# B's attention as a near part of two blocks and a far part by remainders of four, o by rows, p not divided

## The chip, the cores and the metric

One core of a Trainium2 chip runs the kernel. The time is the device time of one execution in microseconds (us); lower is better. The engines have names in the profile: PE is TensorE (matrix products and transposes), PEld its weight load, DVE is VectorE, ACT is ScalarE, POOL is GpSimd, SP is SyncE, which here issues every DMA.

## The reference

One decoder block over 1024 tokens of width 1024, in float32. Two mixers share one input projection; their outputs are normed, joined and projected; then an MLP of width 4096 follows.

```
proj = (rms_norm(x) * (1 + sc_a) + sh_a) @ w_in         # width 2304
A: 8 query heads on 2 key heads of 64; query t sees keys t-127..t; a sink logit joins the denominator
B: 8 heads of 64; three branches (128, 1), (512, 4), (2048, 16):
   branch (w, d): query t attends keys t, t-d, ..., t-(w//d)*d
   outputs are joined with weights proportional to the branches' softmax denominators
mixed = concat(rms_norm(oa), rms_norm(ob)); y = mixed @ w_out
x = x + gt_a * rms_norm(y)
h = rms_norm(x) * (1 + sc_m) + sh_m
x = x + gt_m * rms_norm(relu(h @ w_up)**2 @ w_down)
```

Since the branches are joined by their denominators, B is one softmax over all keys in which a key counts once for each branch that has it.

## The kernel before, in words

Every float32 product is made of pairs of a high and a low part (names with `hl`, `oh`/`ol`, `ph`), most with three matmuls. A planner written in the kernel itself goes through all steps ahead of time with costs of its own (`op`, `pe_op`, `load`), and so fixes the order of instructions on each engine; `prefer` orders the kinds of TensorE's steps. On the chip each engine runs its list in that order.

The stages of the program are, in the profile's time: loads and the first unit (0 to 46 us); the input projection in six units of 384 columns (units 0 to 3 hold two heads of B each, units 4 and 5 hold four query heads and one key head of A), each over eight blocks of 128 tokens, with attention between the projection matmuls (46 to 436); the output projection over eight token blocks (436 to 546); a transition (546 to 574); the MLP (574 to 1136) and a tail. The projection's matmuls are L766, L767 and L769 (`pj`). After a tile, `evac` splits v (`v_hl`), applies the rotary turn, and transposes q (`pq`, L719) and k (`pk`, L731) to `qt` and `kt`.

B's attention (`s_b`) takes one head and two query blocks at a time and all key blocks up to them: scores (L1022), a mask that adds the logarithm of how many branches have the key (L1040, with the minimum `mn` of the negated scores), exp with its sum `den` (ACT, L1047), the reciprocal (DVE, L1050), and the division of p (POOL, L1052). A's (`s_a_`) does the same for four heads and two key blocks, with the sink (L1101 to L1107) and the division at L1111 on POOL or DVE. `t_pv` transposes p (L1125, L1128 for B, L1132 for A), splits it into `ph` (ACT L1139, DVE L1143), and multiplies with v as the weights: the columns that stream are the queries, so o comes out with its head dimension on the partitions (B: L1156, L1159, L1161; A: L1167). High and low halves are added (L1187 and L1191, L1202 and L1207) and o goes to DRAM.

The output projection (`out_block`) loads o (L1318), splits it (`oh` L1331, `ol` L1334), squares it and sums over the partitions with `pm_o` (L1347) for the two norms `rab`, and multiplies with w_out (L1373 to L1375); then the post-norm, the residual and the pre-norm of the MLP (`xn`, L1427) and its transposes (`px`, L1436). `kring`, `qring`, `vring` are the rings of buffers of keys, queries and v; `Res` counts their places.

Of the kernel before, what the change touches and what calls it, by code (L numbers as in the profile page):

```python
# [57 lines left out]
CW_MB = HEAD  # L58
CW_MA = CW_MB + 1024
CW = CW_MA + 256  # L60


def _host(inputs):

    h = {n: np.ascontiguousarray(inputs[n]) for n in _INS}
    c = np.zeros((P, CW), np.float32)
    c[:, CW_C:CW_C + KC] = inputs["c"][0].reshape(P, KC)
    c[:, CW_SINK:CW_SINK + 8] = inputs["sink_a"]
    b = inputs["b_ada"][0].reshape(48, P)
    c[:, CW_COL:CW_COL + 56] = np.concatenate(  # L70
        [inputs["g_attn_pre"][0].reshape(8, P), inputs["g_mlp_pre"][0].reshape(8, P), b[0:16], b[24:40],
         inputs["g_mix_a"][0].reshape(4, P), inputs["g_mix_b"][0].reshape(4, P)]).T
    h["positions"] = np.ascontiguousarray(inputs["positions"][0].reshape(TB, P).T)
    _constants(c)
    h["consts"] = c
    return h


def _constants(c):
    c[:, CW_ID:CW_ID + P] = np.eye(P, dtype=np.float32)  # L80
    p = np.arange(P)[:, None]
    d = p + 896 - np.arange(1024)[None, :]
    mult = ((d >= 0) & (d <= 128)).astype(int)
    mult += (d >= 0) & (d <= 512) & (d % 4 == 0)
    mult += (d >= 0) & (d % 16 == 0)
    neg = np.array([BIG, 0.0, -np.log(2.0), -np.log(3.0)], np.float32)
    c[:, CW_MB:CW_MB + 1024] = neg[mult]
    d = p + P - np.arange(256)[None, :]
    c[:, CW_MA:CW_MA + 256] = np.where((d >= 0) & (d <= 127), 0.0, BIG)
    c[:, CW_F:CW_F + 8] = np.array(INV_FREQ, np.float32)[None, :]  # L90
# [217 lines left out]
def hybrid_block(ctx: ExitStack, tc: tile.TileContext, x, positions, w_ada, b_ada, g_attn_post, w_in, w_out,  # L308
# [33 lines left out]
    WR, WS, NP, NV, NK, NQ, NT, NO = 10, 5, 4, 21, 10, 12, 2, 6  # L342
# [4 lines left out]
    r_v, r_k, r_q, r_p, r_ph, r_ot, r_tmp = Res(NV), Res(0), Res(0), Res(NP), Res(NT), Res(NO), Res(1)  # L347
# [20 lines left out]
    nsink = const.tile([P, 8], F32, name="nsink")  # L368
    ssq = const.tile([P, TB], F32, name="ssq")
# [4 lines left out]
    o_dram = [dram.tile([KC, P, 256], F32, name=f"o_dram{i}") for i in range(4)]  # L374
# [16 lines left out]
    class Tok:  # L391
        pass

# [269 lines left out]
    toks, kts, e_posted = {}, {}, {}  # L663
    acc_at = [(pj, "pj", r_pj)] * 2 + [(po, "o", r_o)] + [(psp, "s", r_s)] * 2 + [(pt, "t", r_t)] * 2 + [(px, "x", r_x)]

    def evac(u, tb, get_ps, done, r_bank):
# [6 lines left out]
        t.v = []  # L673
        b = {}

        def f_vh():
            t.v += [vring.tile([P, 2, 64], F32R, name="v_hl", tag="v") for _ in range(nv)]
            for h in range(nv):
                A.copy(t.v[h][:, 0], get_ps()[:, n + 64 * h:n + 64 * h + 64])
        e2 = op("ACT", nv * t_as(64), f_vh, [done], takes=[(r_v, nv)], prio=2)  # L680

        def f_vl():
            for h in range(nv):
                V.tensor_tensor(t.v[h][:, 1], get_ps()[:, n + 64 * h:n + 64 * h + 64],
                                t.v[h][:, 0].bitcast(F32), ALU.subtract)
        t.e_v = op("DVE", nv * t_dv(64), f_vl, [e2], prio=2)
# [27 lines left out]

        def f_pq():
            t.q = [qring.tile([P, P], F32R, name="qt", tag="qt") for _ in range(nq)]
# [3 lines left out]
        e7 = pe_op("post", 0.056 * nq, f_pq, [e6, e_idr], takes=[(r_x, 1), (r_q, nq)])  # L720

        def f_q():
            for h in range(nq):
                A.mul(t.q[h][:], b["pq"][:, h].bitcast(F32), -0.125)
        t.e_q = op("ACT", nq * t_ps(128), f_q, [e7], gives=[(r_x, 1)], prio=2)

        def f_pk():
            b["pk"] = px.tile([P, 4, P], F32R, name="pk", tag="x")
# [3 lines left out]
        need_k = (2 if tb % 2 == 0 else 0) if u < 4 else (2 if tb == 0 else 1 if tb < TB - 1 else 0)  # L732
        e8 = pe_op("post", 0.112 * nk, f_pk, [e6], takes=[(r_x, 1), (r_k, need_k)], gives=[(r_sp, 1)])

        def get_k(i, h):
            if (u, i, h) not in kts:
                kts[u, i, h] = kring.tile([P, 2, 256], F32R, name="kt", tag="kt")
            return kts[u, i, h]

        def f_k(fn):  # L740
            def f():
                for h in range(nk):
                    kt = get_k(tb // 2, h) if u < 4 else get_k(tb, 0)
                    o = tb % 2 * P if u < 4 else P
                    fn(kt[:, :, o:o + P], b["pk"][:, 2 * h:2 * h + 2].bitcast(F32))
            return f

        def posted():
            st.posted = u * TB + tb + 1
        twice = u >= 4 and tb < TB - 1  # L750
        t.e_k = op(("ACT", "DVE"), (nk * t_ps(256), nk * t_dv(256)), (f_k(A.copy), f_k(V.tensor_copy)), [e8],
                   gives=[] if twice else [(r_x, 1)], prio=2, after=posted)
        t.e_kn = None
        if twice:
            def f_kn(fn):
                return lambda: fn(get_k(tb + 1, 0)[:, :, 0:P], b["pk"][:, 0:2].bitcast(F32))
            t.e_kn = op(("ACT", "DVE"), (t_ps(256), t_dv(256)), (f_kn(A.copy), f_kn(V.tensor_copy)), [t.e_k],
                        gives=[(r_x, 1)], prio=2)
# [98 lines left out]
    def open_attention():  # L857
        if e_rope.t is None or any(x.t is None for x in e_hl.values()):
            return False
        nonlocal kring, qring, pprob, pth, opool, adp, mask_a, mask_b, e_mask  # L860
# [4 lines left out]
        qring = pool("qring", NQ, **kw)  # L865
        pprob = pool("pprob", NP, **kw)
        pth = pool("pth", NT, **kw)
        opool = pool("op", NO, **kw)
        adp = pool("adp", 1, **kw)
        r_k.give(sc.clk["PE"], NK)  # L870
        r_q.give(sc.clk["PE"], NQ)
        masks = mkp.tile([P, 1280], F32, name="masks")
        e_mask = load(lambda: nc.sync.dma_start(masks[:], consts[:, CW_MB:CW_MB + 1280]), 655360, prio=-20)
        mask_b = masks[:, 0:1024]
        mask_a = masks[:, 1024:1280]
# [4 lines left out]
    kring = qring = pprob = pth = opool = adp = mask_a = mask_b = e_mask = None  # L880
# [84 lines left out]
    def feed_ada():  # L965
        if st.d > 1.0 + ada.i * 4.1 / NADA and ada.i < NADA:
# [5 lines left out]
    items = [(u, tp, h) for u in range(4)  # L972
             for tp, h in ((0, 0), (0, 1), (1, 0), (1, 1), (2, 0), (3, 0), (2, 1), (3, 1))]
    items += [(u, qb) for u in (4, 5) for qb in range(TB)]
    UB = 2 * (0.218 * 20 + 0.107 * 36 + 0.43 * 10)
    UA = 0.86 * 8 + 0.43 * 15 + 0.43 * 15

    def need(it):
        return it[0] * TB + (2 * it[1] + 2 if it[0] < 4 else it[1] + 1)

    def count(it):
        return it[1] + 1 if it[0] < 4 else (2 if it[1] else 1)
# [3 lines left out]

    def emit_item(i):
        it = items[i]
        rec = Tok()
        rec.p = []  # L990
        (s_b if it[0] < 4 else s_a_)(i, it, rec)
        nch = count(it)
        for ch in range(nch):
            t_pv(i, it, rec, ch, nch)

    def s_b(i, it, rec):
        u, tp, h = it
        shared = tp < 2
        rec.e_p = []
        rec.held = 1 if shared else 2  # L1000
        for qi in range(2):
            qb = 2 * tp + qi
            W = (qb + 1) * P
            last_mn = None
            b = {}
            for c0 in range(0, W, 512):
                m = c0 // 512
                cw = min(512, W - c0)
                end = c0 + cw == W

                def f_s(c0=c0, cw=cw, m=m, qi=qi, qb=qb, W=W, b=b):
                    if m == 0:
                        if qi == 0 or not shared:
                            rec.tile = pprob.tile([P, 1024], F32, name="p_sb", tag="p")
                        off = 2 * tp * P + P if shared and qi else 0
                        rec.p.append(rec.tile[:, off:off + W])
                        b["mn"] = small.tile([P, 2], F32, name="mn", tag="mn")
                    s = b["s", m] = psp.tile([P, 512], F32, name="s_ps", tag="s")
                    for b0 in range(0, cw, 256):
                        w = min(256, cw - b0)  # L1020
                        for hl in range(2):
                            T.matmul(s[:, b0:b0 + w], toks[u, qb].q[h][:],  # L1022
                                     kts[u, (c0 + b0) // 256, h][:, hl, :w], start=(hl == 0), stop=(hl == 1))
                d = 0.218 * -(-cw // 256)
                deps = [toks[u, j].e_k for j in range(2 * tp, 2 * tp + 2)] + [toks[u, qb].e_q]
                slot = 1 if m == 0 and (qi == 0 or not shared) else 0
                done = end and qi == 1

                def after(d=d, done=done):
                    progress(d, it)  # L1030
                    if done:
                        st.s_items = i + 1
                gives = []
                if done:
                    gives = [(r_q, 2)] + ([(r_k, 4)] if tp == 3 else [])
# [939 lines left out]
```

## Time and profile before

| what | value |
|---|---|
| runs | 1173.84 us median of 3 (1173.43 to 1175.96) |
| profiled execution | 1175.14 us, of which the span is 1173.3 |
| granted TensorE clock, mean | 0.993 |
| busy: PE, DVE, ACT, POOL | 1137.0, 871.9, 677.6, 239.3 us |
| projection and attention | 46 to 436 us |
| output projection, transition | 436 to 546, 546 to 574 us |
| MLP | 574 to 1136 us |

An engine's share is its busy time over the span. A line of a group has the source line, the engine, the operation, what it writes and reads, the shapes, the count, then busy us and mean ns, then idle time ahead of it and what ended that. A row of the timeline has its start, its length and the count of like instructions in it. A matmul's recorded length holds its pipeline, so two neighbouring ones overlap.

### The profile page before, as it was taken

Reading aid. Unit: us, or ns where it says so; the run is one execution under the profiler, and the core shown is the slowest. Engines: PE = TensorE matmul, PEld = TensorE weight load, DVE = VectorE, ACT = ScalarE, POOL = GpSimd, SP = SyncE. Lnnn points to the kernel's source line nnn. Section 1 sums busy time; section 2 is a strip of 40 time slices with the busy share of each in tenths; the row PEclk is TensorE's granted clock in tenths of the full one; section 3 lists DMA queues with packets and bytes.
Section 4 is the critical chain, followed back from the end, with each engine's and each line's share of the span. In section 5 each row is a group of like instructions: output and inputs, shape, how many; then the busy total and the mean of one; then the engine's idle time right before and its main releaser. Section 6 shows DMA issues by size and latency. Waiting matters only on the chain.

```text
span 1173.3 us, 17394 instructions
## 1 busy us (share of the span) xinstructions
PE 1137.0 (97%) x6042; PEld 987.6 (84%) x6042; DVE 871.9 (74%) x1765; ACT 677.6 (58%) x1421; POOL 239.3 (20%) x295
## 2 busy tenths in 40 slices
PE   8999999999999999999899999999999999999996
PEld 7889999999988878887688888888888888888885
DVE  7876787776788896668969764499653796636998
ACT  7966676666666786666667524473225733246542
POOL 2053464554654451112000000000000000000002
PEclk9999999999999999999999999999999999999998
DMA  9712234132223224465485147922258411575103
GB/s 327 209 64 78 74 87 117 53 104 71 70 70 104 79 73 130 172 202 218 150 333 181 36 150 243 357 84 90 100 214 306 143 50 54 202 283 201 37 19 144
DMA packets 96488, 166.54 MB, mean 142 GB/s; under 512 B 11408, under 2 KB 48400, under 8 KB 96400
## 3 DMA queue, kind: packets, MB, share of 16 engines
q1 hardware_dynamic: 96400, 165.42, 42.0%
q8 instruction: 48, 0.79, 0.3%
q14 instruction: 40, 0.33, 0.1%
HBM read 137.08 MB, written 28.31 MB: 141 GB/s over the span
## 4 chain that ended last, share of the span: by engine, by line
PE 77%; DVE 11%; issue 4%; ACT 3%; POOL 1%; DMA 1%; DVEq 0%; POOLq 0%; SPq 0%; ACTq 0%
PE mlp_ps L1798 16%; PE mlp_ps L1799 16%; PE mlp_ps L1797 16%; PE pj L766 4%; PE pj L767 4%; PE pj L769 4%; PE s_ps L1022 3%; PE o_ps L1156 2%; PE pt_ps L1125 1%; DMA w_st<-in_w_in 1%; PE y_ps L1373 1%; PE y_ps L1375 1%; PE y_ps L1374 1%; PE s_ps L1073 1%; PE pt_ps L1128 1%
## 5 line engine op out<-in xcount | busy, mean ns | idle before, releaser
L1797 PE MATMUL mlp_ps<-hw 128*128 128x512 f32 x896 | 349.7, 390 | 1.1 <-ACT hw L1559 1.1
L1798 PE MATMUL mlp_ps<-hw 128*128 128x512 f32 x896 | 348.7, 389 | 1.1 <-DVE hw L1565 1.1
L1799 PE MATMUL mlp_ps<-hw 128*128 128x512 f32 x896 | 348.6, 389 | 0.0
L1797 PEld LDWEIGHTS mlp_ps<-hw 128*128 128x128 f32 x896 | 168.2, 188 | 36.9 <-ACT hw L1559 1.6
L1798 PEld LDWEIGHTS mlp_ps<-hw 128*128 128x128 f32 x896 | 168.2, 188 | 36.6 <-DVE hw L1565 1.4
L1799 PEld LDWEIGHTS mlp_ps<-hw 128*128 128x128 f32 x896 | 168.2, 188 | 34.9
L1568 DVE TENSOR_TENSOR hw<-w,hw 128x1024 fp32r<-128x1024 f32 x96 | 114.6, 1219 | 95.1 <-ACT hw L1561 93.0
L1561 ACT CAST hw<-w 128x1024 fp32r<-128x1024 f32 x96 | 97.4, 1046 | 129.9 <-PE mlp_ps L1799 93.2
L1897 POOL TENSOR_TENSOR st<-st,nhalf 128x1 f32<-128x1 f32 x8 | 7.7, 977 | 602.0 <-DVE st L1895 602.0
L766 PE MATMUL pj<-w_hl,hw 128*128 128x384 f32 x320 | 119.1, 372 | 0.0
L767 PE MATMUL pj<-w_hl,hw 128*128 128x384 f32 x320 | 108.7, 340 | 0.5 <-DVE w_hl L506 0.5
L769 PE MATMUL pj<-w_hl,hw 128*128 128x384 f32 x320 | 108.9, 340 | 0.0
L1561 ACT CAST hw<-u 128x1024 fp32r<-128x1024 f32 x48 | 48.6, 1052 | 64.6 <-PE mlp_ps L1799 64.6
L1143 DVE TENSOR_TENSOR ph<-pt_ps,ph 128x512 fp32r<-128x512 f32 (+1 forms) x110 | 68.9, 644 | 18.6 <-ACT ph L1139 18.0
L1568 DVE TENSOR_TENSOR hw<-u,hw 128x1024 fp32r<-128x1024 f32 x48 | 57.0, 1218 | 18.2 <-ACT hw L1561 18.2
L1139 ACT CAST ph<-pt_ps 128x512 fp32r<-128x512 f32 (+1 forms) x110 | 59.8, 562 | 12.9 <-PE pt_ps L1128 8.8
L1052 POOL TENSOR_SCALAR p_sb<-p_sb,den 128x128 f32<-128x128 f32 (+3 forms) x64 | 49.1, 773 | 87.4 <-DVE den L1050 49.8
L1855 DVE TENSOR_TENSOR yacc<-yacc,mlp_ps 128x512 f32<-128x512 f32 x96 | 62.2, 681 | 3.3 <-PE mlp_ps L1799 3.3
L767 PEld LDWEIGHTS pj<-w_hl,hw 128*128 128x128 f32 x320 | 61.0, 191 | 2.1 <-DVE w_hl L506 0.8
L766 PEld LDWEIGHTS pj<-w_hl,hw 128*128 128x128 f32 x320 | 60.7, 190 | 1.6 <-issue 0.5
L769 PEld LDWEIGHTS pj<-w_hl,hw 128*128 128x128 f32 x320 | 60.6, 189 | 0.0
L1047 ACT ACTIVATE p_sb<-p_sb,mn 128x128 f32<-128x128 f32 (+3 forms) x64 | 50.0, 782 | 17.4 <-DVE mn L1040 13.5
(206 smaller groups left out, 2201.0 us busy)
## 6 DMA issues: line engine op xcount, KB each, us to landing
hw<-s_dram SPq DMA_DIRECT2D x84, 512.0 KB, 4.4
wa_st<-in_w_ada SPq DMA_DIRECT2D x32, 512.0 KB, 4.2
w<-in_w_up SPq DMA_DIRECT2D x32, 512.0 KB, 5.1
w<-in_w_down SPq DMA_DIRECT2D x32, 512.0 KB, 7.5
s_dram<-hw SPq DMA_DIRECT2D x28, 512.0 KB, 4.5
x_sb<-in_x SPq DMA_DIRECT2D x16, 512.0 KB, 5.4
wa<-in_w_ada SPq DMA_DIRECT2D x32, 256.0 KB, 6.1
w_st<-in_w_in SPq DMA_DIRECT2D x32, 192.0 KB, 3.8
```

The lines of the kernel that those rows point to most:

```text
L766: T.matmul(ps, hw[:, tb, 0, t], w[:, 0], start=(k == 0), stop=False)
L767: T.matmul(ps, hw[:, tb, 0, t], w[:, 1], start=False, stop=False)
L769: T.matmul(ps, hw[:, tb, 1, t], w[:, 0], start=False, stop=(k == KC - 1))
L1047: A.activation(rec.p[qi], rec.p[qi], AF.Exp, bias=b["mn"][:, m:m + 1], scale=-1.0, accum_out=b["den"][:])
L1139: A.copy(b["ph"][:, 0, :w], b["pt"][:, :w])
L1143: V.tensor_tensor(b["ph"][:, 1, :w], b["pt"][:, :w], b["ph"][:, 0, :w].bitcast(F32), ALU.subtract)
L1561: A.copy(out[j][0], flat(src[j]))
L1568: V.tensor_tensor(out[j][1], flat(src[j]), out[j][0].bitcast(F32), ALU.subtract)
L1797: T.matmul(ps[m][:], sh, mh, start=starts and k == 0, stop=False, **kw)
L1798: T.matmul(ps[m][:], sh, ml_, start=False, stop=False, **kw)
L1799: T.matmul(ps[m][:], sl, mh, start=False, stop=k == 3, **kw)
L1855: e = op("DVE", t_dv(512), lambda: V.tensor_tensor(y(), y(), ps[m][:], ALU.add), [e, ml.e_y[tb, n]], gives=gives, prio=1)
```

## The change

Within each block of 128 tokens the rows are ordered by their remainder of four: the rows of x and of the output are loaded and stored so, and the positions and masks are made for it. B's keys are then held in one tile of 2048 columns for half of the tokens (512), by remainder, so that a remainder's 128 keys of a half lie side by side.

B's softmax is cut in two parts, each with its own minimum and sum. The near part of a query block has its own and the previous block (branch 1: 15 blocks of keys a head). The far part takes 128 queries of one remainder in a half of the sequence, against the keys of the same remainder of that half and of the one before (branches 2 and 3, 12 blocks a head). Before there were 36 a head. v of B is stored to DRAM and loaded again by remainder (`v_dram`, `vf`), the far queries stand in a tile `qf`.

p is no longer divided. In p times v the block of p is now the weight, and v streams: 128 columns (high and low of v) for the high part of p, 64 for the low one, for each head and key block, so that o comes out by rows of tokens. The sums of the far part go through DRAM (`fs_dram`), `far_weights` and `a_weights` make factors `wts` for each row and head, and the output projection multiplies o by them, adds the far part, and transposes o (`pxo`) for w_out. The sums of squares come from ACT's accumulation, without `pm_o`. The rings become smaller, the junk tile of the squares goes, and the tile of `xn` is taken at the post-norm's squares instead.

```diff
-    WR, WS, NP, NV, NK, NQ, NT, NO = 10, 5, 4, 21, 10, 12, 2, 6
+    WR, WS, NP, NV, NK, NQ, NF, NT, NO = 10, 4, 4, 8, 3, 6, 2, 2, 3
...
-            nc.sync.dma_start(x_t[tb][:], x[tb * P:(tb + 1) * P])
+            nc.sync.dma_start(x_t[tb][:], rows(x, tb))
...
+                nc.sync.dma_start(v_dram[u][half_][:, 32 * c:32 * c + 32],
+                                  t.v[:].rearrange("p h s d -> p (h s d)").bitcast(F32))
+                    nc.sync.dma_start(vfs[ub][:].bitcast(F32), v_dram[u][half_][:].rearrange("r p n -> p r n"))
...
-            e = op("DVE", 0.08, lambda b=b: V.reciprocal(b["den"][:], b["den"][:]), [e], prio=0)
-            rec.e_p.append(op("POOL", t_pts(W),
-                              lambda b=b, qi=qi: G.tensor_scalar(rec.p[qi], rec.p[qi], b["den"][:], 1.0,
-                                                                 ALU.mult, ALU.mult), [e], prio=1))
...
-                for s2 in range(2):
-                    T.matmul(o[:, :256], v0, ph[:, s2, 0:256], start=(ch == 0 and s2 == 0), stop=False)
...
-                for s2 in range(2):
-                    T.matmul(o[:], vv, ph[:, s2], start=(ch == 0 and s2 == 0), stop=(last and s2 == 1))
...
+            for ci in range(2):
+                for kb in range(r.nk):
+                    v = r.v(kb, ci)
+                    kw = dict(stop=kb == r.nk - 1, skip_group_check=True)
+                    T.matmul(rec.o[:, 2 * j + ci], b["ph"][:, 0, at(kb, ci)], v.rearrange("p s d -> p (s d)"),
+                             start=kb == 0, **kw)
+                    T.matmul(rec.o[:, 2 * j + ci, 0:64], b["ph"][:, 1, at(kb, ci)], v[:, 0], start=False, **kw)
...
+        e1 = op("DVE", t_dv(D), by_head(V, lambda: b["ot"][:], wts[:, tb, 0:16]), [el, e_wb, e_wa[tb]], prio=2)
...
+                    T.transpose(b["po", g][:, k], b["ot"][:, kk * P:kk * P + P], ident)
...
-        if st.d < 5.99 and st.d - st.a < LEAD:
+        if st.d < 5.99 and st.d - st.a < (LEAD if st.d < 5 else 0.2):
```

TensorE in the A stage, before: one item's p times v (L1167, two matmuls for a key block with the columns of four heads), between transposes of p (L1132) and scores (L1073).

```order
L766 MATMUL pj<-w_hl,hw 128x384
L767 MATMUL pj<-w_hl,hw 128x384
L769 MATMUL pj<-w_hl,hw 128x384
L1132 MATMUL pt_ps<-head,p_sb 128x128 x4
L1073 MATMUL s_ps<-kt,qt 128x256 x8
L1167 MATMUL o_ps<-ph,v_hl 128x512 x2
L1132 MATMUL pt_ps<-head,p_sb 128x128 x4
L1167 MATMUL o_ps<-ph,v_hl 128x512 x2
```

TensorE in the A stage, after: p times v of half an item, two heads and two key blocks, in pairs of L1180 (high part of p) and L1182 (low part); L748 is the transpose of q and L811 to L814 are the projection.

```order
L748 MATMUL pq<-ident_r,sp 128x128 x4
L1180 MATMUL o_ps<-v_hl,ph 128x128
L1182 MATMUL o_ps<-v_hl,ph 128x64
L1180 MATMUL o_ps<-v_hl,ph 128x128
L1182 MATMUL o_ps<-v_hl,ph 128x64
L1180 MATMUL o_ps<-v_hl,ph 128x128
L1182 MATMUL o_ps<-v_hl,ph 128x64
L1180 MATMUL o_ps<-v_hl,ph 128x128
L1182 MATMUL o_ps<-v_hl,ph 128x64
L811 MATMUL pj<-w_hl,hw 128x384
```

Where four matmuls of 512 columns served the two key blocks of an item's four heads, sixteen of 128 and 64 columns now do.

DVE in the A stage, before: between the masks of one item (L1089) stand the sink and the reciprocal of the item ahead (L1101, L1106, L1107), on which its division by POOL or DVE (L1111) and then its transposes wait.

```order
L1143 TENSOR_TENSOR ph<-pt_ps,ph 128x512
L1101 TENSOR_TENSOR es_5789<-mn_5692,head 128x4
L1143 TENSOR_TENSOR ph<-pt_ps,ph 128x512
L1089 ISA p_sb,mn_5782<-s_ps,masks,nsink 128x128
L1089 ISA mn_5782 128x1
L1106 TENSOR_TENSOR den_5693<-den_5693,es_5789 128x4
L1107 RECIPROCAL den_5693<-den_5693 128x4
```

DVE in the A stage, after: the sink and the reciprocal make `wts` (L1262, L1266, L1267) for the output projection.

```order
L1262 TENSOR_TENSOR wts<-mn,head 128x8
L1170 TENSOR_TENSOR ph<-pt_ps,ph 128x512
L1266 TENSOR_TENSOR wts<-wts,den 128x8
L1267 RECIPROCAL wts<-wts 128x8
L1170 TENSOR_TENSOR ph<-pt_ps,ph 128x512
```

They stand among the same splits of p, but no step of the item's own attention waits for them now, and no L1111 is left.

More of the change, by code (lines that the diff above doesn't have):

```diff
@@ L713, in evac @@
         e6 = op("DVE", t_dv(64 * nq) + t_dv(128 * nk), f_l, [e5, t.e_v], gives=[(r_bank, 1)], prio=2)
+        first = isb and ub not in e_qf
+        new_k = first if isb else tb == 0
+        e_qf.setdefault(ub, [])
         def f_pq():
-            t.q = [qring.tile([P, P], F32R, name="qt", tag="qt") for _ in range(nq)]
+            t.q = [qring.tile([P, 2, P], F32R, name="qt", tag="qt") for _ in range(nq // 2)]
+            if first:
+                qfs[ub] = qfring.tile([P, 2, 4, P], F32R, name="qf", tag="qf")
             b["pq"] = px.tile([P, 4, P], F32R, name="pq", tag="x")
@@ L1133, in t_pv @@
-        d = w / P * 0.113
-        et = pe_op("t", d, f_t, rec.e_p, takes=[(r_t, 1), (r_ph, 1)],
-                   gives=[(r_p, rec.held)] if last else [], after=lambda: progress(d, it))
+            b["pt"] = pt.tile([P, 512], F32, name="pt_ps", tag="t")
+            for kb in range(r.nk):
+                for ci in range(2):
+                    T.transpose(b["pt"][:, at(kb, ci)], r.p[:, ci, r.k0 + kb * P:r.k0 + kb * P + P], ident)
+        d = 0.216 * r.nk
+        et = pe_op("t", d, f_t, r.e_p, takes=[(r_t, 1), (r_ph, 1)], gives=[(r_p, 1)], after=lambda: progress(d, it))
@@ L1180, in t_pv @@
+        if not j:
             return
         ob = {}
[L1182 to L1217 removed]
@@ new lines, in f_o, with f_st @@
+        def f_o():
+            ob["o"] = opool.tile([P, 4, 64], F32, name="ot", tag="ot")
+            A.copy(ob["o"][:], rec.o[:, :, 0:64])
+        e = op("ACT", t_ps(256), f_o, [ep], takes=[(r_ot, 1)], prio=0)
+        e = op("DVE", t_dv(256), lambda: V.tensor_tensor(ob["o"][:], ob["o"][:], rec.o[:, :, 64:128], ALU.add), [e],
+               gives=[(r_o, 1)], prio=0)
+        u, kind = it[:2]
+        both = []
+        for x_ in range(1 if kind == "a" else 2):
+            def f_st(x_=x_):
+                o = ob["o"][:] if kind == "a" else ob["o"][:, 2 * x_:2 * x_ + 2]
+                if kind == "a":
+                    to = o_dram[it[2]][:, 256 * (u - 4):256 * (u - 4) + 256]
+                elif kind == "n":
+                    to = o_dram[2 * it[2] + x_][:, 512 + P * u:512 + P * u + P]
+                else:
+                    to = of_dram[it[2]][2 * it[3] + x_, :, P * u:P * u + P]
+                nc.sync.dma_start(to, o.rearrange("p h d -> p (h d)"))
+            key = (it[2] if kind == "a" else 2 * it[2] + x_ if kind == "n" else ("f", it[2]), i, x_)
+            e_o[key] = load(f_st, 131072 if kind == "a" else 65536, [e], prio=-5,
+                            gives=[(r_ot, 1)] if kind == "a" or x_ else [])
@@ L1338, in f_sum @@
-        def f_sum():
-            sq = b["sq"] = b["ot"].rearrange("p (a b) t -> p a b t", a=2)
-            V.tensor_tensor(sq[:, :, 0:2], sq[:, :, 0:2], sq[:, :, 2:4], ALU.add)
-            V.tensor_tensor(sq[:, :, 0], sq[:, :, 0], sq[:, :, 1], ALU.add)
-        e = op("DVE", t_dv(512) + t_dv(256), f_sum, [e], prio=2)
-        def f_pm():
-            b["pm"] = px.tile([P, 2], F32, name="pm_o", tag="x")
-            for i in range(2):
-                T.matmul(b["pm"][:, i:i + 1], b["sq"][:, i, 0], ones[:, 0:1], start=True, stop=True)
-            b["rab"] = small.tile([P, 2], F32, name="rab", tag="rab")
```

589 lines of the change are left out of this document (308 added, 281 removed).

## Prediction

> **What bounds the kernel now.** I read the page's busy times first, then the chain that ended last, then the busy time of each engine by stage, the waits of TensorE, and last the timeline where single matmuls can be priced.
>
> ```profile
> PE 1137.0 (97%) x6042; PEld 987.6 (84%) x6042; DVE 871.9 (74%) x1765; ACT 677.6 (58%) x1421; POOL 239.3 (20%) x295
> ...
> PE 77%; DVE 11%; issue 4%; ACT 3%; POOL 1%; DMA 1%; DVEq 0%; POOLq 0%; SPq 0%; ACTq 0%
> ```
>
> TensorE is busy for 97% and carries 77% of the chain, so the first question is what the change does to TensorE's own work, and the second how much of its idle time can go. By stage (length, then busy us of PE, weight load, DVE, ACT, POOL, then granted clock and DMA share):
>
> ```profile
> 46.00:345.00 299.00, 293.41 (x2076) 282.73 (x2074) 220.30 (x763) 199.94 (x605) 155.39 (x177) 0.99 0.29 81
> 345.00:436.00 91.00, 83.04 (x525) 77.15 (x523) 80.52 (x267) 68.50 (x227) 43.84 (x59) 0.96 0.28 83
> 436.00:546.00 110.00, 107.63 (x527) 88.13 (x526) 74.70 (x136) 74.07 (x125) 18.74 (x30) 1.00 0.50 169
> 546.00:574.00 28.00, 23.05 (x107) 18.48 (x107) 25.23 (x40) 18.18 (x29) 4.91 (x2) 1.00 0.25 101
> 574.00:1136.00 562.00, 561.65 (x2474) 464.33 (x2475) 402.50 (x420) 267.00 (x355) 0.00 (x0) 1.00 0.48 168
> ...
> 150.00:325.00 175.00, 173.17 (x1245) 167.56 (x1243) 126.71 (x431) 112.09 (x334) 103.26 (x111) 1.00 0.30 83
> ```
>
> The rows are: projection with B's attention, with A's attention, output projection, transition, MLP. The change touches nothing in the MLP. Up to 546 TensorE idles 5.6 us (299.00 - 293.41), 8.0 us and 2.4 us; the transition idles 5.0 us. The clock columns add what a busy TensorE loses: 0.01 of 299 and 0.04 of 91, 3.0 + 3.6 = 6.6 us. In the A stage DVE is busy 80.5 of 91 us, nearly as long as TensorE. The longest waits up to 546 and the one of the transition:
>
> ```profile
> PE pq L719 <- DVE sp L711: 3.7, 3, 2.2
> PE o_ps L1167 <- ACT p_sb L1094: 2.1, 1, 2.1
> PE o_ps L1167 <- DVE ot L1207: 2.0, 1, 2.0
> ...
> 560.28 1.09 PE L1436 MATMUL px<-head,xn 128*128 128x128 f32 x8 [3.05 <-ACT xn L1427]
> ```
>
> The first three are of the A stage and wait for DVE or for what feeds it; each is followed by a stretch of lower clock.
>
> **The price of a TensorE instruction.** A matmul's recorded duration (390 ns for 512 columns) holds its pipeline; the price is the distance from start to start in a full stream.
>
> ```profile
> 376.26 0.62 PE L1167 MATMUL o_ps<-ph,v_hl 128*128 128x512 f32 x2
> 376.72 0.34 PE L766 MATMUL pj<-w_hl,hw 128*128 128x384 f32 x1
> ...
> 377.25 0.64 PE L1073 MATMUL s_ps<-kt,qt 128*128 128x256 f32 x4
> 377.73 0.45 PE L719 MATMUL pq<-ident_r,sp 128*128 128x128 f32 x4
> ...
> 380.33 0.60 PE L1132 MATMUL pt_ps<-head,p_sb 128*128 128x128 f32 x4
> 380.69 0.42 PE L766 MATMUL pj<-w_hl,hw 128*128 128x384 f32 x1
> 380.95 0.33 PE L767 MATMUL pj<-w_hl,hw 128*128 128x384 f32 x1
> 381.12 0.34 PE L769 MATMUL pj<-w_hl,hw 128*128 128x384 f32 x1
> ...
> 382.81 0.56 PE L1073 MATMUL s_ps<-kt,qt 128*128 128x128 f32 x4
> 383.20 0.39 PE L766 MATMUL pj<-w_hl,hw 128*128 128x384 f32 x1
> 383.43 0.34 PE L767 MATMUL pj<-w_hl,hw 128*128 128x384 f32 x1
> ...
> 230.68 0.95 PE L928 MATMUL ada_ps<-ones,ada_acc 128*128 128x1 f32 x8
> 231.49 0.36 PE L1022 MATMUL s_ps<-kt,qt 128*128 128x256 f32 x1
> ```
>
> 512 columns: 0.46 / 2 = 0.23 us. 256 columns: 0.48 / 4 = 0.12. Four transposes: 0.36, and the matmul behind them takes 0.26 where the next takes 0.17, so 0.45 / 4 = 0.11. Four of 128 columns: 0.39, with 0.23 against 0.17 behind them, 0.45 / 4 = 0.11. And eight of a single column: 0.81 / 8 = 0.10. So below 256 columns a matmul does not get cheaper: one column costs what 128 cost. Each has a weight load of its own (6042 of both kinds on the page), and that is what is left to set the price.
>
> The Trainium skill, "TensorE: Matmul & The Clock Gate", section "LDWEIGHTS (loading the stationary operand)", gives a load time of about 107 ns for 128 columns, which these rows bear out; its section "Back-to-back issue gap" gives about 81 ns for a matmul of 128 columns, which they do not.
>
> **The change, term by term.** The counts of before that change:
>
> ```profile
> L1022 PE MATMUL s_ps<-kt,qt 128*128 128x256 f32 x256 | 44.7, 293 | 0.0
> L1156 PE MATMUL o_ps<-ph,v_hl 128*128 128x256 f32 x160 | 36.2, 301 | 2.6 <-DVE ph L1143 2.2 <-DVE ot L1191 0.3
> L1125 PE MATMUL pt_ps<-head,p_sb 128*128 128x128 f32 x160 | 31.5, 278 | 0.4 <-DVE sk L712 0.4
> L1128 PE MATMUL pt_ps<-head,p_sb 128*128 128x128 f32 x128 | 27.3, 275 | 0.0
> L1167 PE MATMUL o_ps<-ph,v_hl 128*128 128x512 f32 x60 | 20.2, 424 | 4.1 <-ACT p_sb L1094 2.1 <-DVE ot L1207 2.0
> L1161 PE MATMUL o_ps<-ph,v_hl 128*128 128x256 f32 x96 | 19.2, 282 | 0.0
> L1073 PE MATMUL s_ps<-kt,qt 128*128 128x256 f32 x112 | 18.6, 292 | 0.1
> L1132 PE MATMUL pt_ps<-head,p_sb 128*128 128x128 f32 x120 | 17.3, 272 | 0.0
> L1022 PE MATMUL s_ps<-kt,qt 128*128 128x128 f32 x64 | 11.1, 255 | 0.0
> L1159 PE MATMUL o_ps<-ph,v_hl 128*128 128x128 f32 x64 | 11.0, 254 | 0.0
> ...
> L1347 PE MATMUL pm_o<-ones,o_sb 128*128 128x1 f32 x32 | 4.5, 243 | 1.2 <-ACT xn L1427 0.4 <-DVE o_sb L1341 0.3
> ...
> L1073 PE MATMUL s_ps<-kt,qt 128*128 128x128 f32 x16 | 2.2, 262 | 0.0
> ```
>
> *TensorE.* Before: 624 of 256 columns (256 + 112 + 160 + 96) x 0.12 = 74.9; 144 of 128 columns (64 + 64 + 16) x 0.11 = 15.8; 60 x 0.23 = 13.8; 408 transposes of p x 0.11 = 44.9; 32 x 0.11 = 3.5. Together 152.9 us. After, by the program: 208 scores of 256 columns = 25.0; 256 scores of 128 columns = 28.2 (64 of near keys, 192 of far); p times v in 336 matmuls of 128 columns = 37.0 and 336 of 64 columns = 37.0; 336 transposes of p = 37.0 and 64 new ones of o in the output projection = 7.0. Together 171.2 us. So B has a quarter fewer key blocks (27 for 36 a head), yet TensorE's work grows by 18.3 us. The reason is the form: v was the weight and one load served 256 or 512 columns of queries; now a block of p is the weight and serves 128 or 64 columns. For A, which is computed over the same blocks, p times v alone goes from 13.8 to 120 x 0.11 + 120 x 0.11 = 26.4 us. The 64-column form is not in the trace; its ends are 0.10 (one column) and 0.11 (128), which moves the sum by 3.4 us. It is on the path everywhere, since TensorE is the bound.
>
> *Idle time of TensorE.* What can be won back by an easier DVE, ACT and POOL is the idle up to 436, 5.6 + 8.0 = 13.6, and the clock, 6.6: 20.2 us. Some idle stays: the calm stretch of 150 to 325 has 1.8 us in 175, about 1%, which over 390 us is 4.1. I take 20.2 - 4.1 = 16.1 us won. From below it could be nothing, if the new, shorter items wait in other places; from above 27.6, if the 7.4 us of output projection and transition go too. I take a value towards the upper side because DVE loses these, and two dozen smaller groups, with nothing of like size in their place before 436:
>
> ```profile
> L1111 DVE TENSOR_SCALAR p_sb<-p_sb,den 128x256 f32<-128x256 f32 x9 | 7.7, 894 | 0.1
> ...
> L1050 DVE RECIPROCAL den<-den 128x1 f32<-128x1 f32 x64 | 9.8, 156 | 8.7 <-ACT p_sb L1047 8.7
> ...
> L1052 POOL TENSOR_SCALAR p_sb<-p_sb,den 128x128 f32<-128x128 f32 (+3 forms) x64 | 49.1, 773 | 87.4 <-DVE den L1050 49.8
> ```
>
> *Costed at nothing.* The 0.16 + 0.77 us of reciprocal and division leave the way from exp to transpose; projection matmuls stand there now and hide it (no row has PE waiting for POOL's p_sb), so removing it gains only through the idle above. SP gets 482 issues for 428: 32 stores of v, 8 reloads of 512 KB, the exchange of far sums. In the order 79 TensorE instructions stand between the last key transposes of the first half and the first matmul on reloaded v, at least 79 x 0.10 = 7.9 us; DMA's share is 0.29 there. Uncovered, each of the 8 reloads could stop TensorE for some us, with scores and projection queued behind it in the fixed order. The exps of B come in more pieces, but ACT is busy 200 of 299 us. In the output projection DVE gets a multiply of 1024 and additions instead of a split and sums; at 74.7 of 110 us it has room, and without it a few us would show. The tile of xn is taken earlier; the last block's 3.05 us wait stays, give or take 1.
>
> *Sum.* 18.3 - 16.1 = +2.2 us. The profiled execution took 1175.14 us (span 1173.3), 1.3 over the median of the runs; on the median, 1173.84 + 2.2 = 1176.
>
> **Rivals.**
> (a) The short matmuls cost less in the new bursts than the nearest rows: with the 64-column form at half of the 128-column one, 336 x 0.055 = 18.5 us go and the time is 1176 - 18.5 = 1157.5. For it: bursts of equal matmuls are longer than before. Against it: eight single columns in a row took 0.10 each. By the skill's 81 ns for both short forms the sum would be lower by (928 - 144) x 0.029 = 22.7 us, an estimate from that page, 1153.
> (b) Faster, by one mechanism: DVE was what held TensorE. With it relieved no wait up to 436 is left, the clock never drops, and the ends of output projection and transition gain some. Between 20.2 and 27.6 us are won back, 1173.84 + 18.3 - 24 = 1168. It decides once over 20.6 us are won. For it: the waits of 2 us name DVE, and 80.5 of 91 us is a full engine. Against it: 5.0 us of the transition end in the chain of the last output block (ACT xn L1427), which keeps its steps.
> (c) Clearly slower: the won-back time is half, 8 us or less, because in a fixed order each p-times-v burst waits for the low part of p (the 2.2 us at L1156 do so today), because the ring of keys has three places, or because reloaded v comes late: 1173.84 + 18.3 - 8 = 1184, and 1192 with nothing won.
> (d) That the change doesn't do what it says I can exclude by the counts of the order.
>
> **How the numbers follow.** No change can be told within about 0.2%, 2.3 us, so 1171.5 to 1176.2. My forecast, 1176 with its own range of 1172 to 1180, gets 0.40 (0.25 of it inside the 0.2%, 0.15 slower), (a) 0.08, (b) 0.24, (c) 0.28. Faster: 0.08 + 0.24 = 0.32; same 0.25; slower 0.15 + 0.28 = 0.43. The range for 8 in 10 goes from the lower part of (b), 1165, to the middle of (c), 1188; outside lie (a) and the end of (c).
>
> **What would show it.** TensorE's instructions of B and A at 0.11 us in the new p-times-v bursts (0.44 us for two pairs) show the price right; 0.3 us or less shows (a). The A stage's idle and clock: 1% idle and 1.00 is my forecast, 8 us idle is (c). DVE in that stage should be well under 80 of 91 us. Waits of matmuls on reloaded v (vf) should be absent. The prediction fails most simply if the projection-and-attention part ends before its old 436 us, or more than 10 us later.

## The result, and the profile after

The changed kernel takes 1301.54 us (median of 4 runs, 1294.7 to 1511.47) against 1173.99: a ratio of 1.1064, 95% interval 1.1019 to 1.1109. Timed again beside the experiments it was 1294.8 against 1175.42, 1.1033 (1.0979 to 1.1087). The forecast was 1176, 1165 to 1188. A ratio with its interval is estimated from single runs and can differ a little from the quotient of the medians. One of the four runs, 1511.47 and the one profiled with the first result, had a clock of about 0.75 from end to end, so the ratio leaves it out and the profile shown below is of another execution of the same kernel, 1306.67 us.

The page's busy times and its row of the granted clock, after:

```profile
PE 1186.3 (91%) x6310; PEld 1039.9 (80%) x6310; DVE 833.1 (64%) x1677; ACT 671.0 (51%) x1448; POOL 176.4 (14%) x195
...
PEclk7698899999999988787899999999999999999995
```

TensorE went from 97% to 91% busy. Its own work grew, as forecast, but that is not where some 120 us went: it idles at the start, and again in the output projection, where the clock row shows a second valley. By stage (length, busy PE, weight load, DVE, ACT, POOL, clock, DMA share), after:

```profile
0.00:106.00 106.00, 74.08 (x362) 65.87 (x363) 58.40 (x143) 57.09 (x97) 16.50 (x27) 0.81 0.51 159
106.00:474.00 368.00, 364.29 (x2653) 357.81 (x2652) 235.48 (x874) 238.28 (x776) 119.88 (x119) 0.97 0.36 106
...
474.00:652.00 178.00, 131.39 (x591) 108.00 (x590) 77.52 (x144) 76.79 (x166) 26.47 (x39) 0.82 0.35 115
652.00:1275.00 623.00, 616.23 (x2710) 508.23 (x2708) 455.62 (x507) 297.42 (x408) 12.51 (x9) 0.99 0.45 160
1275.00:1305.00 30.00, 0.30 (x2) 0.00 (x0) 6.06 (x12) 1.45 (x4) 1.08 (x2) 0.56 0.24 94
```

The stages are cut at the last matmul of each kind in the timeline: of the first unit (`acc`), of the projection (`pj`), of the output projection (`y_ps`), of the MLP (`mlp_ps`). The table has the lengths between these for all kernels, in us of the profiled execution (for the changed kernel one of 1306.67 us and for b_perm8 one of 1203.36, both above the median), and the median of the runs. The kernels were timed in four groups, each beside its own runs of before (1175.42, 1173.87, 1173.78 and 1175.87).

| kernel | to last acc | to last pj | to last y_ps | to last mlp_ps | to the end | median |
|---|---|---|---|---|---|---|
| before | 71.2 | 356.5 | 116.1 | 619.7 | 9.7 | 1173.84 |
| changed | 106.1 | 368.2 | 177.9 | 622.9 | 29.8 | 1294.8 |
| a_x4 | 79.3 | 366.6 | 173.5 | 622.6 | 29.0 | 1274.2 |
| a_all4 | 77.8 | 369.4 | 127.3 | 622.4 | 17.4 | 1215.9 |
| b_perm (4) | 105.6 | 355.6 | 116.2 | 619.7 | 9.7 | 1208.7 |
| b_perm8 | 97.8 | 356.1 | 116.2 | 621.7 | 9.7 | 1194.4 |
| b_perm16 | 78.8 | 353.5 | 116.2 | 620.6 | 9.7 | 1179.5 |
| a_nat | 71.5 | 360.0 | 129.1 | 623.3 | 10.2 | 1196.2 |
| a_nat_lo128 | 72.1 | 360.4 | 127.7 | 622.4 | 10.2 | 1195.7 |
| b_pvA | 72.1 | 360.2 | 118.3 | 620.6 | 9.7 | 1182.8 |
| a_xtnat | 105.7 | 367.6 | 135.6 | 623.9 | 29.8 | 1261.7 |
| a_far4 | 104.3 | 358.8 | 156.5 | 623.8 | 29.1 | 1279.7 |
| a_nat_early | 71.4 | 360.6 | 124.0 | 622.5 | 10.2 | 1190.7 |

Changed against before, in order: +34.9, +11.7, +61.8, +3.2, +20.1, together 131.6 us, the difference of the two spans (the medians are 119.4 apart). Start, output projection and end have 117 of it, and in each of them there are transfers that put rows in the order of the remainder. What TensorE waits for in the changed kernel, with the longest ones:

```profile
PE pxo L1409 <- DVE rs_t L1481: 29.6, 6, 10.8
PE pxt L599 <- ACT x_sb L591: 25.2, 3, 10.6
PE pxo L1409 <- DVE ph L1170: 9.3, 1, 9.3
PE pxo L1409 <- DVE o_sb L1388: 6.5, 1, 6.5
```

The second row is the start: the transposes of x wait for x. The other three are the new transposes of o. The engine that a row names is here only the last in the queue: rs_t is a short step that DVE does just ahead. What the transposes lack is the far part, by the far tile's own waits and its waiters (two lines of that tile's view; the first is its buffer waiting for the transfer, the second its multiply on POOL waiting):

```profile
  DMA far_sb<-of_dram: 66.7, 8
...
  POOL far_sb L1388: 65.1, 7
```

And at the end the queue that issues the transfers takes 25.42 us for nine stores of the output, after, where the last eight before lie within 10.78 us, most of it between the issues (0.33 us for each issue; after, eight of the nine take 2.4 to 4.9 us):

```profile
1267.70 25.42 SPq L1975 DMA_DIRECT2D out_x<-x_sb  x9
```

```profile
1159.79 10.78 SPq L1905 DMA_DIRECT2D out_x<-x_sb  x8
```

### The profile page after: what moved, and what is told of

Read it like the earlier page. It is cut to its first block, busy times and chain, and to the rows that moved or that the text cites. A ratio compares the mean times of both kernels' runs of the same rounds, so it can differ in the third digit from the quotient of the medians.

```text
span 1509.7 us, 17759 instructions
## 1 busy us (share of the span) xinstructions
PE 1425.1 (94%) x6310; PEld 1125.6 (75%) x6310; DVE 846.5 (56%) x1677; ACT 676.1 (45%) x1448; POOL 170.6 (11%) x195
## 4 chain that ended last, share of the span: by engine, by line
PE 85%; DMA 8%; DVE 2%; SPq 1%; issue 1%; ACT 1%; POOL 0%; DVEq 0%; POOLq 0%; ACTq 0%
PE mlp_ps L1867 16%; PE mlp_ps L1869 16%; PE mlp_ps L1868 16%; PE pj L811 5%; PE pj L814 4%; PE pj L812 4%; DMA far_sb<-of_dram 4%; PE s_ps L1126 4%; PE o_ps L1180 3%; PE pt_ps L1160 3%; DMA wa<-in_w_ada 3%; PE o_ps L1182 2%; PE y_ps L1444 1%; PE y_ps L1445 1%; PE y_ps L1443 1%; PE pk L783 1%
## 5 line engine op out<-in xcount | busy, mean ns | idle before, releaser
L1867 PE MATMUL mlp_ps<-hw 128*128 128x512 f32 x896 | 411.7, 459 | 2.0 <-ACT hw L1629 2.0
L1868 PE MATMUL mlp_ps<-hw 128*128 128x512 f32 x896 | 409.8, 457 | 1.5 <-DVE hw L1635 1.5
L1869 PE MATMUL mlp_ps<-hw 128*128 128x512 f32 x896 | 408.7, 456 | 0.0
L1867 PEld LDWEIGHTS mlp_ps<-hw 128*128 128x128 f32 x896 | 178.1, 199 | 79.0 <-ACT hw L1629 2.5
L1868 PEld LDWEIGHTS mlp_ps<-hw 128*128 128x128 f32 x896 | 178.6, 199 | 78.3 <-DVE hw L1635 2.0
L1869 PEld LDWEIGHTS mlp_ps<-hw 128*128 128x128 f32 x896 | 179.2, 200 | 76.1
L811 PE MATMUL pj<-w_hl,hw 128*128 128x384 f32 x320 | 137.2, 429 | 0.0
L814 PE MATMUL pj<-w_hl,hw 128*128 128x384 f32 x320 | 125.5, 392 | 0.0
L812 PE MATMUL pj<-w_hl,hw 128*128 128x384 f32 x320 | 123.6, 386 | 0.0
L1925 DVE TENSOR_TENSOR yacc<-yacc,mlp_ps 128x512 f32<-128x512 f32 x96 | 65.5, 687 | 37.2 <-PE mlp_ps L1869 37.1
L1170 DVE TENSOR_TENSOR ph<-pt_ps,ph 128x512 fp32r<-128x512 f32 (+1 forms) x96 | 58.6, 620 | 36.8 <-ACT ph L1166 36.3
L1142 ACT ACTIVATE p_sb<-p_sb,mn 128x256 f32<-128x256 f32 (+1 forms) x128 | 62.6, 491 | 29.3 <-DVE mn L1138 29.2
L812 PEld LDWEIGHTS pj<-w_hl,hw 128*128 128x128 f32 x320 | 69.6, 217 | 2.2 <-issue 0.7
L811 PEld LDWEIGHTS pj<-w_hl,hw 128*128 128x128 f32 x320 | 68.7, 215 | 2.1 <-issue 0.8
L1166 ACT CAST ph<-pt_ps 128x512 fp32r<-128x512 f32 (+1 forms) x96 | 50.2, 532 | 41.8 <-PE pt_ps L1160 41.2
L1180 PE MATMUL o_ps<-v_hl,ph 128*128 128x128 f32 x240 | 66.6, 322 | 0.0
L814 PEld LDWEIGHTS pj<-w_hl,hw 128*128 128x128 f32 x320 | 64.8, 203 | 2.2
```

The costliest lines, as they stand in the source:

```text
L811: T.matmul(ps, hw[:, tb, 0, t], w[:, 0], start=(k == 0), stop=False)
L812: T.matmul(ps, hw[:, tb, 0, t], w[:, 1], start=False, stop=False)
L814: T.matmul(ps, hw[:, tb, 1, t], w[:, 0], start=False, stop=(k == KC - 1))
L1142: A.activation(r.p[:, ci, k0:], r.p[:, ci, k0:], AF.Exp, bias=sums(ci)[0], scale=-1.0, accum_out=sums(ci)[1])
L1180: T.matmul(rec.o[:, 2 * j + ci], b["ph"][:, 0, at(kb, ci)], v.rearrange("p s d -> p (s d)"), start=kb == 0, **kw)
L1867: T.matmul(ps[m][:], sh, mh, start=starts and k == 0, stop=False, **kw)
```

## The experiments

**Which of three causes.** Theory S: a transfer written with the remainder (4) as its slowest dimension runs on few of the 16 DMA engines, and holds up what is queued behind it there. Theory C: the clock. Theory W: TensorE's work.

The changed kernel, run again:

> The changed kernel as it is, for a profile at the usual clock. Theory S (few DMA engines): transfers that put rows in the order of the remainder have 4 as their slowest dimension and run on 4 of the 16 DMA engines; then about 1300 us, with the time lost at the start (x loads, beyond 46 us by 30 to 45 us), in the output projection (far loads) and little in the attention part. Theory C (clock): TensorE's granted clock is lower through the whole program because of the short matmuls; then the MLP is longer than 562 us too. Theory W (work): the loss lies in 46 to 436 us, where TensorE's own work grew.

The MLP has its old length within 3.2 us, so C in its strong form is out, and 11.7 us of 131.6 lie in the attention part, so W is not the main cause.

a_x4, the first loads of x in four transfers of 32 rows:

```diff
+    def by_rest(t, tb, tile_, cs=slice(0, D), back=False):
+        for r in range(4):
+            d = t[tb * P:(tb + 1) * P, cs].rearrange("(a r) d -> r a d", r=4)[r]
+            s_ = tile_[32 * r:32 * r + 32]
+            nc.sync.dma_start(d if back else s_, s_ if back else d)
...
-            nc.sync.dma_start(x_t[tb][:], rows(x, tb))
+            by_rest(x, tb, x_t[tb])
```

> Only the eight first loads of x are cut into four, one for each remainder (32 rows each). Theory S: the start comes back to about 46 us, 1255 to 1275 us. Theories C and W: no change, 1300 us.

1274.2 (ratio 1.0824, 1.0781 to 1.0868), the start 79.3 instead of 106.1 and nothing else moved by more than 5 us; the start did not come all the way back, to 71.2. a_all4 does the same for the second loads of x, the stores of v, the far loads and the stores of the output:

> All transfers with a slowest dimension of 4 (x twice, v's stores, the far loads, the output's stores) are cut into four. Theory S: 1175 to 1195 us, what was predicted for the work plus some time of the queue that issues 216 more transfers. Theories C and W: 1290 us or more.

1215.9 (1.0319, 1.0276 to 1.0361). Two thirds of the loss are gone, though 20 us more than expected stay.

b_perm adds the one suspect to the kernel before:

```diff
-            nc.sync.dma_start(x_t[tb][:], x[tb * P:(tb + 1) * P])
+            nc.sync.dma_start(x_t[tb][:], x[tb * P:(tb + 1) * P].rearrange("(a r) d -> r a d", r=4))
```

> The kernel before, with nothing but its eight first loads of x put in the order of the remainder by one transfer each (the rows of a block are then permuted, so the masks do not fit the tokens; the amount of work is the same). Theory S: 1200 to 1220 us, the start as late as in the changed kernel. Theories C and W: 1174 us.

1208.7 (1.0286, 1.0269 to 1.0302): the start is 105.6 against the changed kernel's 106.1, and every other stage is as before. So this line alone makes the whole loss at the start. The same rows of 4 KB with another slowest dimension (r=16, r=8):

> The kernel before with its eight first loads of x in the order of a remainder of sixteen instead of four: again one transfer of 128 scattered rows of 4 KB, but with 16 as the slowest dimension (the rows are permuted, so the masks do not fit the tokens). Theory S (the slowest dimension of 4 leaves 4 DMA engines): 1174 us, within 3. Rival (scattered rows are slow in themselves): about 1208, as with the remainder of four.

> As the kernel before with its first loads of x in the order of a remainder, now of eight (8 as the slowest dimension). If the slowest dimension is the number of DMA engines: 8 engines, 16 packets of 4 KB each, 2.6 us for a block instead of 1.3 with sixteen and 5.1 with four, so some 8 x 1.3 = 10 us later than with sixteen and 18 to 24 us earlier than with four: 1186 to 1192 us. If only four is a bad case: 1180 us, as with sixteen.

1179.5 (1.0052, 1.0033 to 1.0070) and 1194.4 (1.0152, 1.0131 to 1.0173), both a little above what was expected: the time falls as the slowest dimension grows, so scattered rows alone do not make the loss with four, though 16 is still 5.6 us behind the plain transfer. The share of the DMA engines' time in the first 46 us (the last number but one) is much lower with 8 and 4. Before, then r = 16, 8 and 4:

```profile
0.00:46.00 46.00, 40.51 (x221) 34.14 (x222) 37.72 (x88) 37.46 (x58) 8.67 (x20) 1.00 0.98 316
```

```profile
0.00:46.00 46.00, 34.36 (x174) 28.04 (x175) 30.66 (x75) 30.01 (x49) 7.94 (x20) 0.96 1.02 273
```

```profile
0.00:46.00 46.00, 29.73 (x117) 24.92 (x118) 18.19 (x53) 18.76 (x31) 5.66 (x16) 0.74 0.75 157
```

```profile
0.00:46.00 46.00, 25.96 (x108) 21.13 (x109) 18.09 (x53) 17.23 (x28) 5.12 (x14) 0.78 0.43 132
```

0.98, 1.02, 0.75 and 0.43 of the engines' time, with 316, 273, 157 and 132 GB/s. Nor is it x alone that is slow. What comes behind it in the queue waits too: the first four pieces of w_ada (`wa`), plain transfers in both kernels, take 2.22 us to issue before and 9.04 in b_perm.

```profile
3.05 2.22 SPq L462 DMA_DIRECT2D wa<-in_w_ada  x4
```

```profile
3.59 9.04 SPq L462 DMA_DIRECT2D wa<-in_w_ada  x4
```

The trace does not name the engine of a packet. The Trainium skill, "DMA: Bandwidth & Descriptors", section "Why a DMA increments its semaphore by 16 and not by 1", says that a transfer is spread over the largest number of engines, up to 16, that divides the slowest dimension of both sides; for r = 16, 8 and 4 that is 16, 8 and 4. What the traces do hold is each step of a load's completion semaphore, and it agrees: for the first load of x it steps sixteen times at 5.0 to 5.5 us before, sixteen times at 6.3 to 6.7 with r = 16, eight times at 8.6 to 9.3 with r = 8 and four times at 9.5 to 10.5 with r = 4 (with 8 and 4 after a single step about 1.1 us behind the issue). In the changed kernel it is four as well, at 10.0 to 11.1, and the first far load and the first store of the output step four times too.

The number of engines is not the whole of it. In the first 20 us a packet of 4 KB takes 0.16 us (median) before and with r = 4, but 0.27 with r = 16 and 0.32 with r = 8. With four the packets are as fast as before and only fewer run at a time (some 4.5 against 16 on average between 4.2 and 7.5 us); what 16 loses, and a part of what 8 loses, comes with slower packets, and why these are slower no run shows. In a_x4, which cuts x into four transfers of scattered rows, they take 0.26 us, and its start (79.3) is close to that of b_perm16 (78.8), which issues nothing more than before.

**The output projection.** Two loads there have the remainder in them, x again and the far part. Each is undone alone: a_xtnat loads x in its own order, a_far4 cuts the far loads in four (the edit is that of a_x4, on `ph2.far`).

> The changed kernel with only the second loads of x, those of the output projection, in their own order (the residual's tokens are then in another order than o's). Theory S in numbers: on 4 engines a block's x is 32 packets of 4 KB for each, 32 x 0.16 = 5.1 us, and its far part 32 of 2 KB, about 2.6 us, and the far part is queued behind x; 8 x 5.1 = 41 us less, about 1254 us. Rival (the far load alone is late): within 10 us of the changed kernel, 1285 us or more.

> The changed kernel with only the far loads in four transfers. Theory S: 8 x 2.6 = 21 us less at most, 1274 us, since each still stands behind a load of x on the same four engines. Rival (the far load alone is late): 1245 us or less.

The output projection falls from 177.9 to 135.6 us with x in its own order, and to 156.5 with the far loads cut: 42.3 and 21.4 us, where 41 and 21 were worked out from packets on four engines. In time they are 1261.7 (1.0744, 1.0702 to 1.0785) and 1279.7 (1.0902, 1.0848 to 1.0957). These are 7.7 and 5.7 us above the 1254 and 1274 expected, and far from the times of the rival, that the far load alone is late (1285 or more, 1245 or less). So both loads lie on the stage's chain. Their 63.7 us are not simply added, though: with both undone, in a_all4, the stage falls by 50.6 (177.9 to 127.3) of the 61.8 that it had lost.

**What is left.** a_nat takes x and output in their own order and cuts the rest, so that no transfer on four engines and no extra issues for x are left:

> The changed kernel with x and the output in their own order (one plain transfer each; the masks then do not fit the tokens), v's stores and the far loads in four transfers each. Theory S with a price for the 192 more issues of x and the output: start and tail as long as before (71 us to the last accumulated tile, 10 us behind the last MLP matmul, together 14 us less than with everything in four), 1195 to 1202 us. Rival (start and tail are late for another reason): 1210 us or more. What then is left over 1174, some 21 to 28 us, is TensorE's own work (+20) and what the output projection waits.

1196.2 (1.0212, 1.0168 to 1.0256), start and end as before. The price of the extra issues, which the expectation names, was not measured by itself: at the start the slower packets are a rival for it. The attention and output stages of a_nat, then the same of before:

```profile
71.00:431.00 360.00, 355.89 (x2654) 348.94 (x2653) 234.74 (x875) 237.72 (x776) 119.84 (x119) 1.00 0.39 111
431.00:561.00 130.00, 120.83 (x593) 99.50 (x593) 81.74 (x144) 76.50 (x166) 28.06 (x39) 0.93 0.44 154
```

```profile
71.00:428.00 357.00, 346.93 (x2422) 332.86 (x2422) 272.75 (x943) 241.99 (x762) 180.32 (x216) 0.99 0.27 77
428.00:544.00 116.00, 111.91 (x554) 91.43 (x553) 80.53 (x161) 79.88 (x143) 23.43 (x37) 1.00 0.49 165
```

At the prices of the prediction, taken to three places (0.227, 0.174, 0.118, 0.111 us), the matmuls of the attention stage are worth 337.6 us before and 356.6 in a_nat, +19.0; the rest of its length is 18.9 and 3.4, -15.5. This is the trade that was forecast. Its size hangs on the prices. Read from the rows, TensorE's idle time goes from 10.1 us (357.00 - 346.93) to 4.1, and the three stretches of half clock in before, 3.4 us each, are gone, which is worth 5.1: 11.1 us won, and so 14.6 us more work in a stage that is 3.5 longer. In the output projection the matmuls are worth 109.2 and 110.0, but the rest, idle time and low clock, is 6.9 and 19.1, +12.2.

The A stage of a_nat (its last two units start within 2 us of those of before):

```profile
345.00:431.00 86.00, 86.00 (x646) 85.01 (x645) 64.70 (x220) 59.44 (x183) 19.47 (x17) 1.00 0.28 88
```

a_nat_early frees the far buffer after the addition, with another tile for the squares:

```diff
-                A.activation(ph2.far[:], b["ot"][:, 512 * i:512 * i + 512], AF.Square, scale=512 ** -0.5,
+                A.activation(ph2.junk[:], b["ot"][:, 512 * i:512 * i + 512], AF.Square, scale=512 ** -0.5,
...
-               [e1, e2], prio=2)
+               [e1, e2], gives=[(ph2.r_f, 1)], prio=2)
...
-        es = op("ACT", t_as(512) + AP_COST, f_sq_o(1), [es], gives=[(ph2.r_f, 1), (r_u if late else ph2.r_o, 1)], prio=2)
+        es = op("ACT", t_as(512) + AP_COST, f_sq_o(1), [es], gives=[(r_u if late else ph2.r_o, 1)], prio=2)
```

> As a_nat, but the one buffer of the far part is free after it is added, since the squares go to another tile. If what is left in the output projection (12 us more idle than before) comes from this one buffer: 8 us or more off, 1188 or less. If it comes from the first block at the end of attention and from the low clock behind it: within 3 us of a_nat.

1190.7 (1.0143, 1.0109 to 1.0177), the output projection 5.1 us shorter: between the two expectations. The one far buffer has 5 of the 12 us; for the others the trace offers the wait at the first block (2.6 us) and 10.2 us of half clock behind it (from 440.2 us), which no run took away.

**The price of the short matmuls.** a_nat_lo128 multiplies the low part of p with 128 columns of v instead of 64; b_pvA gives A's p times v in the kernel before the new form.

```diff
-                    T.matmul(rec.o[:, 2 * j + ci, 0:64], b["ph"][:, 1, at(kb, ci)], v[:, 0], start=False, **kw)
+                    T.matmul(rec.o[:, 2 * j + ci], b["ph"][:, 1, at(kb, ci)], v.rearrange("p s d -> p (s d)"),
+                             start=False, **kw)
```

> As a_nat, but the low part of p multiplies both halves of v: 128 columns instead of 64 in 336 matmuls (the product of both low parts is added, as in the kernel before). If the weight load sets the price of a short matmul (0.11 us for either): within 2 us of a_nat. If columns do (0.055 us more for each): 18 us slower. If the low clock after the first attention items lasts because too few columns stream, it is shorter here and the time some us lower than a_nat.

```diff
-                for s2 in range(2):
-                    T.matmul(o[:], vv, ph[:, s2], start=(ch == 0 and s2 == 0), stop=(last and s2 == 1))
+                for h in range(4):
+                    hs = slice(h * P, h * P + P)
+                    T.matmul(o[:, hs], ph[:, 0, hs], vv, start=ch == 0, stop=last, skip_group_check=True)
+                    T.matmul(o[:, h * P:h * P + 64], ph[:, 1, hs], vv[:, 0:64], start=False, stop=last,
+                             skip_group_check=True)
```

> The kernel before with only A's p times v in the new form: the block of p is the weight, 128 columns of v for its high part and 64 for its low part (o's layout is then not what the later steps expect; all other work is the same). By the price of 0.11 us TensorE's work grows by 26.4 - 13.8 = 12.6 us: 1183 to 1188 us if it lies on the path. With 64 columns at half the price it grows by 6: 1178 to 1180. Rival: the A stage hangs on DVE, and nothing shows: 1174 to 1176.

Doubling the columns of 336 matmuls leaves the time where it was, 1195.7 against 1196.2. The third case of the expectation could not be seen, since a_nat already has no low clock after the first attention items. In the trace of a_nat_lo128 eight of 128 columns take 0.84 us (first row to last), 0.105 each:

```profile
120.78 0.22 PE L1181 MATMUL o_ps<-vf,ph 128*128 128x128 f32 x1
120.84 0.28 PE L1183 MATMUL o_ps<-vf,ph 128*128 128x128 f32 x1
...
121.62 0.34 PE L749 MATMUL pq<-ident_r,sp 128*128 128x128 f32 x2
```

In a_nat sixteen, half of them of 64 columns, take 1.70 us, 0.106 each:

```profile
114.60 0.22 PE L1181 MATMUL o_ps<-vf,ph 128*128 128x128 f32 x1
114.66 0.25 PE L1183 MATMUL o_ps<-vf,ph 128*128 128x64 f32 x1
...
116.30 0.66 PE L1161 MATMUL pt_ps<-head,p_sb 128*128 128x128 f32 x4
```

b_pvA is 8.9 us slower than before (1.0074, 1.0055 to 1.0093) for 12.6 us more of matmuls by the price of 0.11, just under the range expected if all of it lies on the path (1183 to 1188). In the profiled executions the span grows by 7.7, of which 3.7 lie before the last `pj` and 2.2 in the output projection (A's last items run on into it). So the new form costs A several us on the path; that idle time took up the rest is not shown.

## Why the prediction was wrong

- **The step that failed** is the part *Costed at nothing*, and within it the transfers. It counted SP's issues, bytes and the reloads of v, and read a DMA share of 0.29 as room. It never priced the loads of x, the far loads and the output's stores in their new order, one transfer each with a slowest dimension of 4, though the change says that rows are loaded and stored so. The runs showed that such transfers run on four engines: the start became 34.9 us longer, the output projection 61.8 and the end 20.1, and undoing them took the changed kernel from 1294.8 to 1196.2. None of the three was among the rivals either: they were taken as they were, and the start's DMA engines, at a share of 0.98, had no room at all.
- **TensorE's work, +18.3 us**: right in sign and near in size. At the prices of the trace it grew by 19.8 (19.0 + 0.8), and the 64-column form, which had no row, costs 0.106. Worked out from idle time and clock instead, the attention stage has 14.6.
- **Idle won back, 16.1 us**: right in kind, and 15.5 in a_nat by the prices, 11.1 by the rows. That the stage grew by 3.5, near the +2.2 of the sum, does not settle the two terms, since an error in one is taken up by the other. The clock's part was put at 6.6 from two-digit columns; the three stretches of 3.4 us are worth 5.1, and one of the three waits of 2 us, at 431.6, is not followed by one. In the changed kernel only 7.3 are won (18.9 to 11.6): a stretch of half clock of 20.5 us lies in this stage there (below). The sign for the A stage, 1% idle at a clock of 1.00, came out in a_nat (86.00 of 86.00 us busy).
- **Output projection and transition at +0 and "give or take 1"**: a second step that failed. Even without the slow transfers a_nat has 12.2 us more of idle time and low clock in the output projection, and transition and MLP are 3.6 longer, so that 1196.2, too, lies outside the range of 1165 to 1188. The single far buffer, which was not looked at, has about 5 of the 12; the cause of the rest stays open.
- **Reloaded v**: right. No wait for the reload of `vf` is among TensorE's waits.
- **Rivals**: (a) is refuted by a_nat_lo128. (c) had the right side, and its late-transfer half the right kind of cause, but at 1184 to 1192 and in the wrong place, v instead of x. (b) did not occur.

With the transfers mended, 1196.2 and 1190.7 are still slower than before. In both of these x and the output keep their own order, so their masks do not fit the tokens; the fastest version that keeps the new order is a_all4, 1215.9. No run pointed to a version that beats 1173.84.

## What to carry to other kernels

Check each transfer that a new order of rows touches for its slowest dimension before anything else: here 4 instead of 128 cost about 100 us, with the bytes unchanged, and it slowed what was queued behind it as well. The DMA share of one stage (0.29) says nothing about room in another (0.98 at the start). And a change that saves products but turns a long stream behind one weight load into short ones can cost more matmul time than it saves: where a matmul of 64 columns takes as long as one of 128, as here, price it by instructions, not by columns.

## What was not expected of the hardware

The low clock can last while TensorE is busy. In a_all4 two waits of 0.6 and 0.8 us at 91 to 93 us stood ahead of a half clock that held for some 20 us, in which TensorE was never idle but did mostly short matmuls and transposes (12 of the 96 were projection matmuls of 384 columns):

```profile
94.00:114.00 20.00, 20.00 (x96) 19.90 (x95) 10.58 (x39) 10.51 (x39) 3.90 (x4) 0.50 0.12 33
114.00:127.00 13.00, 13.00 (x113) 13.00 (x112) 7.57 (x30) 8.38 (x27) 3.93 (x4) 0.98 0.23 62
```

The changed kernel has the like at 121 to 142 us (clock 0.51), a_nat and a_far4 have none there, and in the kernel before each of the three such stretches ahead of the output projection lasted 3.4 us. The attention stage is 366.6 to 369.4 us long in the four kernels with a stretch of 17 to 20 us there (changed, a_x4, a_all4, a_xtnat) and 358.8 to 360.6 in the four without (a_nat, a_nat_lo128, a_nat_early, a_far4). These eight run nearly the same matmuls in this stage, so their shortness alone does not bring the low clock about. That it keeps the clock down once waits have lowered it fits this, but no run tested it.
